# A two-layer decoder trunk on one core: index scores and mixer A's values merged into fewer stages, powers alone on GpSimd

## The chip, the cores and the metric

The kernel runs on one core of a Trainium2 chip. The metric is the device time of one execution in microseconds (us), the median of several runs; lower is better. The granted TensorE clock in the profiled execution is 0.999 of full speed.

## The reference, cut to what matters

Two decoder layers work on 256 positions of width 1024. One layer is:

```
u    = RMSNorm(h)
proj = u @ w_in  -> qa ka va | qi ki wi | qb kb vb | gate_a gate_b
mixer A: iscore = sum_h wi_h * relu(qi_h . ki)   (4 index heads of 64, causal)
         sel    = the 64 best keys of each query
         softmax(qa . ka) over sel, times va       (8 heads of 64, one shared key and value)
mixer B: softmax(q1 . k1) - lam * softmax(q2 . k2), times vb, per-head RMSNorm (4 heads)
h   += (sigmoid(gate_a) * (o_a @ w_a) + sigmoid(gate_b) * (o_b @ w_b)) @ w_out
h   += ConvFFN(RMSNorm(h))                       (2816 wide, causal width 3, GELU gate)
h   += sigmoid(RMSNorm(h) @ w_ple_gate) * (p @ w_ple_proj)
```

The norms inside the mixers (of qa, ka, qb, kb per head, and of mixer B's output per head) are x * (mean(x^2) + eps)^(-1/2).

## The kernel before, in words

The 256 positions are two tiles of 128 (i = 0, 1). Every weight matrix is cut into chunks of 128 x 1024 floats, 128 chunks per layer, which stream in on the SP queue. ScalarE copies a chunk into a rounded high part `wh` (`split_hi`, line 164) and VectorE subtracts to get the low part `wl` (`split_lo`, line 179; in most of the up-projection GpSimd does half of it, line 176). A product is three TensorE products: high times high, high times low, low times high. `gemm_a` (line 337) runs a projection of 512 columns: for each of the eight blocks of the contraction it issues six products (three for each tile) at line 361.

The attention work is hidden between these products. It is written as generators ("threads") that each issue one stage and then yield three numbers: what the stage is charged on TensorE, VectorE and ScalarE. `Side` (line 61) is a planner that runs while the program is written out, not on the chip. `gemm_a` calls `tick` after every two contraction blocks, so after twelve products, which are charged 2.6 us. One tick goes through the threads by priority and skips a thread whose last stage is not yet due (`t[2]`), skips all of them when the planned VectorE is more than 3.5 us behind (`LIMIT_US`), and issues no further stage once the tick's charges on TensorE have passed 2 us (`SIDE_US`, line 86). After the threads, `tick` prepares further weight chunks. All engines execute in the order in which the program issues, so the plan fixes each engine's queue. `side.until` runs threads with no projection between them until a flag is set.

The threads that the change touches, per layer:

- `index_side` (line 493): rotary products for the index heads, transposes, then for each tile one stage of index scores: four products of 64 contraction rows (line 528, two trace instructions to a pair of row halves), two Relu copies (line 531), and a yield. After both, `select_side` is spawned: the weighted sums and the top-64 mask, on VectorE.
- `heads_side` (line 568): rotary products and norms of qb, kb, qa for each tile. `head_ss` (417) squares on ScalarE and sums on VectorE; `rpow` (260) gives (mul * ss + add)^(-1/2) on GpSimd with two instructions, a multiply-add (263) and a power (264).
- `mixer_b` (641), four of them: score maps, normalisation, transposes, products with the values (662), then the output norm: two squares on ScalarE (667), two multiplications by 1/sum on VectorE (670), `rpow` (672), another multiplication by 1/sum (674), and the scaled output (675).
- `mixer_a` (687), four of them in the order `ORDER_A` = (0,1), (1,1), (0,0), (1,0) of (half of the heads, tile): score maps (602, 639), division by the sums (695), transposes (`ptrans`, 626), then as a last stage of its own the products with the values (705) and the split of the result into high and low parts of `o` (709, 710).
- `nxt_side` (970), once, in the last projection of layer 0: transposes (317) of the first half of `h` for the next layer.

PSUM has four accumulators for the projections (`ps_acc`) and four buffers for all side work (`ps_tp`).

After the four gate projections come the two products of mixer B's output with `w_branch_b` (line 754, four ticks in all), then `side.until` for mixer A's flags (755), then the products with `w_branch_a` (768), which read `o` of mixer A.

Of the kernel before, what the change touches and what calls it, by code (L numbers as in the profile page):

```python
# [9 lines left out]
F32 = mybir.dt.float32  # L10
F32R = mybir.dt.float32r
BF16 = mybir.dt.bfloat16
AF = mybir.ActivationFunctionType
ALU = mybir.AluOpType
# [3 lines left out]
P = 128  # L18
L = 256
# [6 lines left out]
EPS = 1e-6  # L26
# [31 lines left out]
NONE = (0.0, 0.0, 0.0)  # L58
# [51 lines left out]
def decoder_kernel(ctx: ExitStack, tc: tile.TileContext, x, xa, pT, ws, fc, tb, gf, rope, out):  # L110
    nc = tc.nc
# [4 lines left out]
    sm = ctx.enter_context(tc.tile_pool(name="sm", bufs=2))  # L116
    T2 = dict(tag="t2", bufs=10)
    ps_acc = ctx.enter_context(tc.tile_pool(name="ps_acc", bufs=4, space=PSUM))
    ps_tp = ctx.enter_context(tc.tile_pool(name="ps_tp", bufs=4, space=PSUM))
    ctx.enter_context(tc.manual_schedule())  # L120
    side = Side()
# [135 lines left out]
    nc.gpsimd.tensor_copy(cmb, cm[:, P:])  # L257


    def rpow(dst, src, mul, add):  # L260
        n = src.shape[-1]
        t = sm.tile([P, 8], F32, name="pw", bufs=4)
        nc.gpsimd.tensor_scalar(t[:, :n], src, mul, add, op0=ALU.mult, op1=ALU.add)
        nc.gpsimd.tensor_tensor(dst, t[:, :n], mhalf[:, :n], op=ALU.pow)  # L264

    def sq_half(ss, hf, tiles=(0, 1)):

# [61 lines left out]
    def split_T_side(srcs, hf, scale, x, flag):  # L329
        for k0 in (0, 2):  # L330
            split_T2(srcs, hf, k0, scale, x)
            yield 0.45, 0.8, 0.3
        flags.add(flag)

    flags = set()
# [78 lines left out]
        else:  # L414
            nc.vector.tensor_add(dst, m1, m2)

    def head_ss(src, n):
        sq = sm.tile([P, 8, 64], F32, name="sq", **T2)[:, :n, :]
        ss = sm.tile([P, 8], F32, name="hss", bufs=3)
        nc.scalar.activation(sq, src, AF.Square)  # L420
        nc.vector.reduce_sum(ss[:, :n], sq, axis=AX.X)
        return ss[:, :n]

    def transposed(srcs, nb, dst):
# [23 lines left out]
    for l in range(DEPTH):  # L448
# [44 lines left out]
        def index_side(pi):  # L493
            kk, iq, wvs = [], [], []
            for i in range(2):
                v = pi[i]
                nc.scalar.activation(va[:, i, :], v[:, 64:128], AF.Copy)
                kki = sm.tile([P, 4, 64], F32, name="kk")
                rope_rows(kki[:, 0:2, :], v[:, 0:64].unsqueeze(1), 1, rt["ka"], i, dup=True)
                rope_rows(kki[:, 2:4, :], v[:, 384:448].unsqueeze(1), 1, rt["i"], i, dup=True)  # L500
                rk = sm.tile([P, 1], F32, name="rk")
                rpow(rk, head_ss(v[:, 0:64].unsqueeze(1), 1), 1.0 / 64, EPS)
                iqi = sm.tile([P, 4, 64], F32, name="iq")
                rope_rows(iqi, v[:, 128:384].rearrange("p (a b) -> p a b", b=64), 4, rt["i"], i)
                nc.scalar.activation(kki[:, 0:2, :], kki[:, 0:2, :], AF.Copy, scale=rk)
                wv = sm.tile([P, 4], F32, name="wv")
                nc.vector.tensor_scalar(wv, v[:, 448:452], 0.0625, None, op0=ALU.mult)
                kk.append(kki.rearrange("p a b -> p (a b)"))
                iq.append(iqi.rearrange("p a b -> p (a b)"))
                wvs.append(wv)  # L510
                yield 0.0, 2.8, 0.0
            pt = ps_tp.tile([P, 2, L], F32, name="tp")
            for j in range(2):
                for i in range(2):
                    nc.tensor.transpose(pt[:, j, i * P:(i + 1) * P], kk[i][:, j * P:(j + 1) * P], ident)
            nc.scalar.activation(kT, pt[:, 0, :], AF.Copy)
            nc.scalar.activation(kiT, pt[:, 1, :], AF.Copy)
            iqT = sm.tile([P, 2, L], F32, name="iqT", **T2)
            transposed(iq, 2, iqT)
            yield 0.9, 0.0, 1.2  # L520
            rels = []
            for i in range(2):
                S = P * (i + 1)
                rel = b4("rel")[:, :, :S]
                ps = [ps_tp.tile([P, 2, L], F32, name="tp") for _ in range(2)]
                for b in range(2):
                    for r in range(2):
                        nc.tensor.matmul(ps[r][:, b, :S], iqT[r * 64:(r + 1) * 64, b, i * P:(i + 1) * P],
                                         kiT[r * 64:(r + 1) * 64, :S], start=True, stop=True)
                for r in range(2):  # L530
                    nc.scalar.activation(rel[:, r:4:2, :], ps[r][:, :, :S], AF.Relu)
                rels.append(rel)
                yield 0.85 * (i + 1), 0.0, 0.9
            side.spawn(select_side(rels, wvs), P_TOPK)

        def select_side(rels, wvs):
# [31 lines left out]
        def heads_side(pr, nm, is_q):  # L568

            rows, rq = [], []  # L570
            for i in range(2):
                v = pr[i].rearrange("p (a b) -> p a b", b=64)
                q = sm.tile([P, 512], F32, name="qr", **T2)
                q3 = q.rearrange("p (a b) -> p a b", b=64)
                r_ = sm.tile([P, 8], F32, name="rq", bufs=6)
                if is_q:
                    rope_rows(q3, v, 8, rt[nm], i)
                    rpow(r_, head_ss(v, 8), 1.0, 64 * EPS)
                else:
                    rpow(r_, head_ss(v, 8), 1.0 / 64, EPS)  # L580
                    rope_rows(q3, v, 8, rt[nm], i)
                    nc.vector.tensor_mul(q3, q3, r_.unsqueeze(2).broadcast_to([P, 8, 64]))
                rows.append(q)
                rq.append(r_.rearrange("p (b r) -> p r b", r=2))
                yield 0.0, (2.8 if nm == "kb" else 2.2), 0.0
            rqs[nm] = rq
            qT[nm] = b4("qT")
            transposed(rows, 4, qT[nm])
            yield 0.9, 0.0, 1.0
            flags.add(nm)  # L590
# [50 lines left out]
        def mixer_b(hq, i):  # L641
# [5 lines left out]
            cf = sm.tile([P, 2], F32, name="cf", bufs=4)  # L647
            nc.vector.reciprocal(rcp, sums)
            nc.vector.scalar_tensor_tensor(cf, rcp[:, 1, :], nlam, sums[:, 0, :], op0=ALU.mult, op1=ALU.mult)
            for m in range(2):  # L650
                nc.vector.scalar_tensor_tensor(pe[:, 2 * m, :], pe[:, 2 * m + 1, :], cf[:, m:m + 1],
                                               pe[:, 2 * m, :], op0=ALU.mult, op1=ALU.add)
# [11 lines left out]
            sq = sm.tile([P, 2, P], F32, name="osq", **T2)  # L664
            ss_ = sm.tile([P, 2], F32, name="oss")
            for m in range(2):
                nc.scalar.activation(sq[:, m, :], po[:, m, :], AF.Square, accum_out=ss_[:, m:m + 1])
            r1 = rcp[:, 0, :]
            for _ in range(2):
                nc.vector.tensor_mul(ss_, ss_, r1)  # L670
            ff = sm.tile([P, 2], F32, name="ff")
            rpow(ff, ss_, 1.0 / P, EPS)
            yield 0.4 * (i + 1), 0.5, 1.6
            nc.vector.tensor_mul(ff, ff, r1)
            nc.vector.tensor_mul(ob[:, i, hq * 256:(hq + 1) * 256].rearrange("p (b c) -> p b c", c=P), po,
                                 ff.unsqueeze(2).broadcast_to([P, 2, P]))
            yield 0.0, 0.4, 0.0
# [9 lines left out]
        def mixer_a(hq, i):  # L687
            while not {"qa", "mask"} <= flags:
                yield NONE
            pe, sums = maps("qa", product_a, i, hq, mask[i])  # L690
            yield 0.9 + 0.9 * i, 0.8 + 0.6 * i, MA + MB * i
            rcp = sm.tile([P, 2, 2], F32, name="rcp", bufs=4)
            nc.vector.reciprocal(rcp, sums)
            for hh in range(4):
                nc.vector.tensor_scalar(pe[:, hh, :], pe[:, hh, :], rcp[:, hh % 2, hh // 2:hh // 2 + 1], None,
                                        op0=ALU.mult)
            yield 0.0, 0.9 + 0.3 * i, 0.0
            pt = ptrans(pe, 4, i)
            yield 0.5 + 0.5 * i, 0.0, 0.5 + 0.5 * i
            nb = i + 1  # L700
            ptv = pt[:, :4 * nb, :].rearrange("p (m r s) t -> p m r s t", r=2, s=nb)
            po = ps_tp.tile([P, 2, L], F32, name="tp")[:, 0, :].rearrange("p (m t) -> p m t", t=P)
            for sb in range(nb):
                for r in range(2):
                    nc.tensor.matmul(po[r * 64:(r + 1) * 64], va[:, sb, :], ptv[:, :, r, sb, :],  # L705
                                     start=sb == 0, stop=sb == i)
            x = o_parts()
            hi, lo = x.two(2 * hq, slice(i * P, (i + 1) * P))
            nc.scalar.activation(hi, po, AF.Copy)
            nc.vector.tensor_sub(lo, po, hi.bitcast(F32))  # L710
            yield 0.85 * nb, 0.4, 0.35
            flags.add(("a", hq, i))

        def o_side():
            while not {("b", hq, i) for hq, i in ORDER_B} <= flags:
# [17 lines left out]
        side.spawn(heads_side(project(C_QA, 512, "q"), "qa", True), 0)  # L733
        for hq, i in ORDER_A:
            side.spawn(mixer_a(hq, i), 1)


        tg = {}
# [227 lines left out]
        if not last:  # L966
            nxt, nss = HL("u"), new_ss()
            g_nxt = fcs[l + 1][:, 0:8]

            def nxt_side():  # L970
                yield from split_T_side([h[:, i, HALF[0]] for i in range(2)], 0, lambda k: g_nxt[:, k:k + 1],
                                        nxt, "n0")
                sq_half(nss, 0)
                yield 0.0, 0.0, 1.1
# [100 lines left out]
```

## Time and profile before

| | |
|---|---|
| time, median of 3 runs (lowest to highest) | 789.85 us (788.91 to 790.34) |
| the profiled execution: time | 788.69 us |
| its span, first to last instruction | 786.9 us |
| TensorE busy | 779.7 us (99%) |
| VectorE busy | 588.6 us (75%) |
| ScalarE busy | 501.3 us (64%) |
| GpSimd busy | 162.7 us (21%) |

Busy shares are unions of instruction times. A product's row in the timeline has its start and its duration; products overlap, so the distance from one start to the next is what a product costs in a stream, and the duration is longer. PE is TensorE, DVE is VectorE, ACT is ScalarE, POOL is GpSimd.

### The profile page before, as it was taken

What the parts mean: (1) busy time and instruction counts of PE and PEld (TensorE: products, weight loads), DVE (VectorE), ACT (ScalarE), POOL (GpSimd) and SP (SyncE); (2) the same over time, 40 slices, a digit from 0 to 9 for tenths busy, and PEclk for the clock granted to TensorE, in tenths of its full rate; (3) what the DMA queues carried; (4) which work ended last, traced back from release to release, by engine and by line L of the source; (5) the groups of instructions that cost most, each with busy time, mean ns of one, the idle gap of its engine ahead of it and who ended that gap; (6) DMA issues with size and microseconds to landing.
All of it is one profiled execution on the core that took longest, in us unless ns stands there. A gap on an engine that the chain in (4) does not pass through costs nothing.

```text
span 786.9 us, 11698 instructions
## 1 busy us (share of the span) xinstructions
PE 779.7 (99%) x4034; PEld 648.1 (82%) x4034; DVE 588.6 (75%) x1128; ACT 501.3 (64%) x886; POOL 162.7 (21%) x162
## 2 busy tenths in 40 slices
PE   9999999999999999999999999999999999999997
PEld 7877886788888888888888778778888888888886
DVE  5987997675887778754687889768668878795643
ACT  5776657455877777553576486565468777773541
POOL 0250300001344442000123213000104444400000
PEclk9999999999999999999999999999999999999999
DMA  9654353462665556656465345445636656558521
GB/s 331 229 174 152 123 193 125 149 228 94 213 211 180 198 192 210 229 162 224 134 195 177 125 142 166 147 135 189 209 119 207 204 176 202 180 180 290 172 96 54
DMA packets 40204, 140.04 MB, mean 178 GB/s; under 512 B 4560, under 2 KB 5200, under 8 KB 40144
## 3 DMA queue, kind: packets, MB, share of 16 engines
q1 hardware_dynamic: 39280, 137.44, 52.8%
q10 hardware_dynamic: 864, 1.84, 0.7%
q8 instruction: 32, 0.52, 0.3%
q14 instruction: 28, 0.23, 0.1%
HBM read 138.22 MB, written 1.05 MB: 177 GB/s over the span
## 4 chain that ended last, share of the span: by engine, by line
PE 91%; DVE 3%; ACT 3%; POOL 1%; issue 1%; DVEq 0%; ACTq 0%
PE acc L361 36%; PE tp L831 21%; PE tp L833 11%; PE acc L932 5%; PE acc L934 5%; PE acc L933 5%; ACT pe L611 2%; PE tp L317 2%; DVE wl L179 2%; PE tp L626 1%; PE tp L705 1%; PE tp L662 1%; PE tp L639 1%; POOL rq L264 1%; PE tp L431 1%
## 5 line engine op out<-in xcount | busy, mean ns | idle before, releaser
L164 ACT ACTIVATE wh<-raw 128x1024 fp32r<-128x1024 f32 x254 | 263.9, 1057 | 38.4 <-PE acc L934 23.4
L179 DVE TENSOR_TENSOR wl<-raw,wh 128x1024 fp32r<-128x1024 f32 x178 | 213.8, 1220 | 27.8 <-ACT wh L164 27.5
L361 PE MATMUL acc<-wh,u 128*128 128x512 f32 (+1 forms) x672 | 215.1, 394 | 0.0
L831 PE MATMUL tp<-u,wh 128*128 128x512 f32 x704 | 177.1, 392 | 0.0
L361 PEld LDWEIGHTS acc<-wh,u 128*128 128x128 f32 x672 | 126.3, 189 | 26.7 <-issue 0.7
L831 PEld LDWEIGHTS tp<-u,wh 128*128 128x128 f32 x704 | 126.3, 189 | 22.3
L361 PE MATMUL acc<-wl,u 128*128 128x512 f32 (+1 forms) x336 | 129.3, 389 | 0.2 <-DVE wl L179 0.2
L176 POOL TENSOR_TENSOR wl<-raw,wh 128x512 fp32r<-128x512 f32 x76 | 98.5, 1296 | 142.8 <-ACT wh L164 60.9
L833 PEld LDWEIGHTS tp<-u,wl 128*128 128x128 f32 x704 | 96.6, 190 | 7.2
L833 PE MATMUL tp<-u,wl 128*128 128x256 f32 x704 | 98.8, 282 | 0.0
L865 DVE SCALAR_TENSOR_TENSOR cv<-tp,fc,cv 128x255 f32<-128x255 f32 (+1 forms) x176 | 84.2, 478 | 3.1
L361 PEld LDWEIGHTS acc<-wl,u 128*128 128x128 f32 x336 | 63.1, 188 | 12.5 <-DVE wl L179 1.0
L860 DVE TENSOR_TENSOR tp<-tp,cl 128x256 f32<-128x256 f32 x88 | 38.0, 432 | 45.8 <-ACT cl L858 45.4
L932 PE MATMUL acc<-wh,g 128*128 128x512 f32 x176 | 68.9, 391 | 0.0
L934 PE MATMUL acc<-wh,g 128*128 128x512 f32 x176 | 68.5, 389 | 0.0
L933 PE MATMUL acc<-wl,g 128*128 128x512 f32 x176 | 68.5, 389 | 0.0
L861 ACT ACTIVATE cv<-tp,fc 128x256 f32<-128x256 f32 x88 | 49.7, 565 | 25.8 <-DVE tp L860 25.3
L278 POOL TENSOR_SCALAR sst<-ss 128x2 f32<-128x2 f32 (+1 forms) x8 | 5.6, 698 | 259.8 <-ACT junk L270 259.6
L175 DVE TENSOR_TENSOR wl<-raw,wh 128x514 fp32r<-128x514 f32 x76 | 53.6, 705 | 0.0
L858 ACT ACTIVATE cl<-tp 128x256 f32<-128x256 f32 x88 | 33.6, 382 | 28.7 <-PE tp L833 28.6
L611 ACT ACTIVATE pe<-tp,nb,rq 128x256 f32<-128x256 f32 (+1 forms) x64 | 31.8, 528 | 18.0 <-DVE nb L608 12.2
L361 PE MATMUL acc<-wh,o 128*128 128x512 f32 x128 | 42.5, 399 | 0.0
(174 smaller groups left out, 946.4 us busy)
## 6 DMA issues: line engine op xcount, KB each, us to landing
raw<-ws SPq DMA_DIRECT2D x254, 512.0 KB, 3.5
raw<-ws SPq DMA_DIRECT2D x4, 256.0 KB, 5.1
h<-x SPq DMA_DIRECT2D x2, 512.0 KB, 7.1
gb<-gf ACTq DMA_DIRECT2D x2, 512.0 KB, 4.7
out<-h SPq DMA_DIRECT2D x3, 256.0 KB, 2.0
x<-xa SPq DMA_DIRECT2D x2, 256.0 KB, 3.9
px<-pT ACTq DMA_DIRECT2D x2, 256.0 KB, 2.7
tbl<-tb SPq DMA_DIRECT2D x1, 256.0 KB, 6.9
```

Source lines behind the costliest of these rows:

```text
L164: nc.scalar.activation(wh, raw, AF.Copy)
L175: nc.vector.tensor_sub(wl[:, a], raw[:, a], wh[:, a].bitcast(F32))
L176: nc.gpsimd.tensor_tensor(wl[:, b], raw[:, b], wh[:, b].bitcast(F32), op=ALU.subtract)
L179: nc.vector.tensor_sub(wl, raw, wh.bitcast(F32))
L361: nc.tensor.matmul(acc[i][:, :n], a, w, start=q == 0 and j == 0, stop=q == nk - 1 and not any(t[0] == i for t in todo[n_ + 1:]))
L831: nc.tensor.matmul(acc, wh[:, k, :], u.pair(k), start=k == 0, stop=False)
L833: nc.tensor.matmul(acc[:, 0, :], wl[:, k, :], u.hi(k), start=False, stop=k == KD - 1)
L861: nc.scalar.activation(c, pu, AF.Identity, bias=w[:, 3:4], scale=w[:, 2:3])
L865: nc.vector.scalar_tensor_tensor(c[:, sh:], pu[:, :L - sh], w[:, 2 - sh:3 - sh], c[:, sh:], op0=ALU.mult, op1=ALU.add)
L932: nc.tensor.matmul(acc[i], a, wh, start=k == 0, stop=False)
L933: nc.tensor.matmul(acc[i], a, wl, start=False, stop=False)
L934: nc.tensor.matmul(acc[i], b, wh, start=False, stop=k == NF - 1)
```

## The change

Four edits, in both layers except the last:

1. `rpow` keeps only the power on GpSimd. Its multiply-add goes: the factor moves into the scale of the square on ScalarE, the addend is a new small VectorE addition in `head_ss`. In `mixer_b` the factor moves into the square as well; the two multiplications by 1/sum and the one after the power go, and instead eps * sum^2 is worked out once and added to the sum of squares.
2. `index_side` issues the scores of both tiles and yields once.
3. `mixer_a` ends with its transposes. A new thread `values_a(i)`, one per tile, waits for both halves of the heads and issues all their products with the values, then the splits.
4. `nxt_side` yields once, charged 2.8 us of VectorE, before its first transposes.

```diff
-    def rpow(dst, src, mul, add):
-        n = src.shape[-1]
-        t = sm.tile([P, 8], F32, name="pw", bufs=4)
-        nc.gpsimd.tensor_scalar(t[:, :n], src, mul, add, op0=ALU.mult, op1=ALU.add)
-        nc.gpsimd.tensor_tensor(dst, t[:, :n], mhalf[:, :n], op=ALU.pow)
+    def rpow(dst, src):
+        nc.gpsimd.tensor_tensor(dst, src, mhalf[:, :src.shape[-1]], op=ALU.pow)
...
-    def head_ss(src, n):
+    def head_ss(src, n, scale, eps):
...
-        nc.scalar.activation(sq, src, AF.Square)
+        nc.scalar.activation(sq, src, AF.Square, scale=scale)
         nc.vector.reduce_sum(ss[:, :n], sq, axis=AX.X)
+        nc.vector.tensor_scalar(ss[:, :n], ss[:, :n], eps, None, op0=ALU.add)
...
                 rels.append(rel)
-                yield 0.85 * (i + 1), 0.0, 0.9
+            yield 2.1, 0.0, 1.8
...
+            es = sm.tile([P, 2], F32, name="es", bufs=4)
+            nc.vector.scalar_tensor_tensor(es, sums[:, 0, :], EPS, sums[:, 0, :], op0=ALU.mult, op1=ALU.mult)
...
-                nc.scalar.activation(sq[:, m, :], po[:, m, :], AF.Square, accum_out=ss_[:, m:m + 1])
-            r1 = rcp[:, 0, :]
-            for _ in range(2):
-                nc.vector.tensor_mul(ss_, ss_, r1)
+                nc.scalar.activation(sq[:, m, :], po[:, m, :], AF.Square, scale=P ** -0.5, accum_out=ss_[:, m:m + 1])
+            nc.vector.tensor_add(ss_, ss_, es)
             ff = sm.tile([P, 2], F32, name="ff")
-            rpow(ff, ss_, 1.0 / P, EPS)
+            rpow(ff, ss_)
             yield 0.4 * (i + 1), 0.5, 1.6
-            nc.vector.tensor_mul(ff, ff, r1)
...
             yield 0.5 + 0.5 * i, 0.0, 0.5 + 0.5 * i
+            pts[hq, i] = pt
+        pts = {}
+        def values_a(i):
+            while not {(0, i), (1, i)} <= set(pts):
+                yield NONE
             nb = i + 1
...
+            for hq in range(2):
+                ptv = pts[hq, i][:, :4 * nb, :].rearrange("p (m r s) t -> p m r s t", r=2, s=nb)
+                po = ps_tp.tile([P, 2, L], F32, name="tp")[:, 0, :].rearrange("p (m t) -> p m t", t=P)
+                for sb in range(nb):
+                    for r in range(2):
+                        nc.tensor.matmul(po[r * 64:(r + 1) * 64], va[:, sb, :], ptv[:, :, r, sb, :],
+                                         start=sb == 0, stop=sb == i)
+                pos.append(po)
             x = o_parts()
+            for hq in range(2):
+                hi, lo = x.two(2 * hq, slice(i * P, (i + 1) * P))
+                nc.scalar.activation(hi, pos[hq], AF.Copy)
+                nc.vector.tensor_sub(lo, pos[hq], hi.bitcast(F32))
+            yield 1.3 * nb, 0.8, 0.35
+            for hq in range(2):
+                flags.add(("a", hq, i))
...
         for hq, i in ORDER_A:
             side.spawn(mixer_a(hq, i), 1)
+        for i in (1, 0):
+            side.spawn(values_a(i), 1)
...
             def nxt_side():
+                yield 0.0, 2.8, 0.0
                 yield from split_T_side([h[:, i, HALF[0]] for i in range(2)], 0, lambda k: g_nxt[:, k:k + 1],
```

## Rows read from the trace of the kernel before

**Rows 1.** The page: TensorE's busy time, and the chain by engine.

```profile
PE 779.7 (99%) x4034; PEld 648.1 (82%) x4034; DVE 588.6 (75%) x1128; ACT 501.3 (64%) x886; POOL 162.7 (21%) x162
...
PE 91%; DVE 3%; ACT 3%; POOL 1%; issue 1%; DVEq 0%; ACTq 0%
```

**Rows 2.** Two stretches: width, busy us of PE, PEld, DVE, ACT, POOL.

```profile
80.00:100.00 20.00, 20.00 (x111) 16.94 (x110) 19.55 (x60) 13.35 (x30) 7.38 (x9) 1.00 0.40 132
760.00:787.00 27.00, 22.59 (x127) 19.53 (x125) 12.27 (x19) 7.64 (x15) 1.97 (x3) 0.96 0.11 40
```

**Rows 3.** Timeline of PE, layer 0's index scores: start us, us, instruction.

```profile
40.79 0.39 PE L361 MATMUL acc<-wl,u 128*128 128x512 f32 x1
41.01 0.39 PE L361 MATMUL acc<-wh,u 128*128 128x512 f32 x1
41.33 0.72 PE L528 MATMUL tp<-kiT,iqT 64*128 64x128 f32 x8
41.98 0.50 PE L361 MATMUL acc<-wh,u 128*128 128x512 f32 x1
42.31 0.39 PE L361 MATMUL acc<-wl,u 128*128 128x512 f32 x1
...
44.61 0.39 PE L361 MATMUL acc<-wh,u 128*128 128x512 f32 x1
44.92 1.13 PE L528 MATMUL tp<-kiT,iqT 64*128 64x256 f32 x8
45.99 1.09 PE L431 MATMUL tp<-ident,qr 128*128 128x128 f32 x8
```

**Rows 4.** Timeline of PE, layer 0's mixer A: transposes and products with values.

```profile
128.79 1.03 PE L626 MATMUL tp<-ident,pe 128*128 128x128 f32 x8
...
137.41 1.08 PE L705 MATMUL tp<-pt,va 128*64 128x256 f32 x8
138.43 0.66 PE L626 MATMUL tp<-ident,pe 128*128 128x128 f32 x4
...
145.69 0.65 PE L705 MATMUL tp<-pt,va 128*64 128x256 f32 x4
146.27 0.50 PE L361 MATMUL acc<-wh,o 128*128 128x512 f32 x1
146.61 0.39 PE L361 MATMUL acc<-wl,o 128*128 128x512 f32 x1
```

**Rows 5.** Timeline of PE where it waits: idle and releaser in brackets.

```profile
61.06 0.98 PE L431 MATMUL tp<-ident,qr 128*128 128x128 f32 x7 [0.21 <-DVE qr L582]
...
125.07 0.27 PE L602 MATMUL tp<-mk,identb 128*128 128x256 bf16 x1 [0.48 <-ACT pe L611]
...
386.44 0.93 PE L317 MATMUL tp<-ident,h 128*128 128x128 f32 x4
```

**Rows 6.** Instructions by line: count | busy us, mean ns | idle before.

```profile
L263 POOL TENSOR_SCALAR pw<-hss 128x8 f32<-128x8 f32 (+1 forms) x16 | 11.3, 708 | 99.5 <-DVE hss L421 79.5 <-DVE rcp L648 20.0
L670 DVE TENSOR_TENSOR oss<-oss,rcp 128x2 f32<-128x2 f32 x16 | 2.4, 158 | 0.9 <-ACT osq L667 0.6
L649 DVE SCALAR_TENSOR_TENSOR cf<-rcp,nlam,sums 128x2 f32<-128x2 f32 x8 | 1.8, 224 | 0.3
L551 DVE MAX8 m<-sc 128x8 f32<-128x128 f32 (+1 forms) x32 | 9.8, 349 | 0.0
L553 DVE MATCH_REPLACE8 sc<-m,sc 128x128 f32<-128x128 f32 (+1 forms) x32 | 10.7, 344 | 0.0
```

**Rows 7.** Timeline of DVE and PE: a low part, and its first use.

```profile
82.34 1.22 DVE L179 TENSOR_TENSOR wl<-raw,wh 128x1024 fp32r<-128x1024 f32 x1
...
85.39 0.39 PE L361 MATMUL acc<-wl,u 128*128 128x512 f32 x1
```

**Rows 8.** Timeline: the last split of mixer A's output in layer 0.

```profile
146.81 0.42 DVE L710 TENSOR_TENSOR o<-tp,o 128x256 fp32r<-128x256 f32 x1 [0.32 <-ACT o L709]
```

More of the change, by code (lines that the diff above doesn't have):

```diff
@@ L501, in index_side @@
                 rk = sm.tile([P, 1], F32, name="rk")
-                rpow(rk, head_ss(v[:, 0:64].unsqueeze(1), 1), 1.0 / 64, EPS)
+                rpow(rk, head_ss(v[:, 0:64].unsqueeze(1), 1, 0.125, EPS))
                 iqi = sm.tile([P, 4, 64], F32, name="iq")
@@ L577, in heads_side @@
                     rope_rows(q3, v, 8, rt[nm], i)
-                    rpow(r_, head_ss(v, 8), 1.0, 64 * EPS)
+                    rpow(r_, head_ss(v, 8, 1.0, 64 * EPS))
                 else:
-                    rpow(r_, head_ss(v, 8), 1.0 / 64, EPS)
+                    rpow(r_, head_ss(v, 8, 0.125, EPS))
                     rope_rows(q3, v, 8, rt[nm], i)
@@ L699, in mixer_a @@
             yield 0.5 + 0.5 * i, 0.0, 0.5 + 0.5 * i
-            nb = i + 1
[L701 to L706, printed above, removed]
-            x = o_parts()
[L708 to L712, printed above, removed]
+            pts[hq, i] = pt
[3 more added lines that the diff above has]
+                yield NONE
+            nb = i + 1
+            pos = []
+            for hq in range(2):
[6 more added lines that the diff above has]
+                pos.append(po)
+            x = o_parts()
+            for hq in range(2):
[5 more added lines that the diff above has]
+                flags.add(("a", hq, i))
         def o_side():
```

## The prediction

> **What bounds the kernel now.** I read the page first. TensorE is busy 779.7 us, 99% of the span, and 91% of the chain that ended last is TensorE [rows 1]; the reader is to see that no other engine's work sets the time, and that an edit pays only where TensorE's own queue gets shorter. Next the stretches: of the 7.2 us in which TensorE is idle (786.9 - 779.7), 4.4 lie in the last 27 us [rows 2], which no edit touches. But a product's duration there overlaps the next one's, so busy time doesn't show a product that starts late. Third, therefore, the timeline of TensorE, read by distances between starts. In a stream of products of 512 columns it is 0.22 to 0.23 us; I take 0.227. Where side work comes between two of them the distances grow, and that is what this change moves.
>
> **Merged index scores.** In [rows 3] tile 0's stage begins 0.32 us after the last projection product (41.01 to 41.33), so 0.09 late; its eight instructions take 0.65; the first product behind it takes 0.33 (41.98 to 42.31), 0.10 too long. Tile 1's stage is again 0.09 late and takes 1.07; eight transposes follow it at once. Their group lasts 1.09, against 1.03 for the same eight begun straight from the projection [rows 4], so 0.06. What a pair of products costs in the stream comes from the values stages [rows 4]: four pairs in 1.02 us (137.41 to 138.43), two pairs in 0.58 (145.69 to 146.27), so 0.22 a pair and 0.14 fixed per stage. A pair of index scores of tile 1 has as many columns, one of tile 0 half: the fixed parts are 0.65 - 4 x 0.11 = 0.21 and 1.07 - 4 x 0.22 = 0.19. One stage less saves 0.09 + 0.20 + 0.06 = 0.35 us per layer. The least is 0.15 (the fixed part stays), the most 0.40 (a way out to the projection goes, 0.10). I take 0.35.
>
> **Merged values.** Before there are four stages per layer, after it two. Two ways in and two fixed parts go: 2 x (0.09 + 0.14) = 0.46. Ways out: before, three lead to transposes (0.06 each) and one to the projection (146.27 to 146.61, 0.34, so 0.11): 0.29; after, two lead to the projection: 0.22. That saves 0.07, together 0.53 per layer, least 0.25 (fixed parts stay), most 0.60.
>
> A rule of the Trainium skill bears on this (TensorEngine Tiling (Array Packing), Key Properties): changing the tiling mode, not just the tile, drains TensorE. The trace agrees that something of the kind is paid at each such border, 0.09 us on the way in. The rule prices only the drain, though; with the 128 cycles that TensorE: Matmul & The Clock Gate gives for a drain (Step-by-step: what each phase is for), an estimate of 0.05 us, the twelve borders that go in two layers would be worth 0.6 us.
>
> Where does the plan put the new stages? By line 86 no further stage is issued once a tick's charges pass 2. In the products with `w_branch_b` a tick before held values (1.7) and one transpose stage (1.0), which passes 2, so each of its four ticks held one values stage, the last just ahead of `w_branch_a`. After the change tile 1's second half (1.0) and both halves of tile 0 (0.5 each) fit in the first of these ticks, tile 1's values (2.6) are alone in the next, tile 0's (1.3) in the third. At least twelve products then stand between the last values and their reader, as now, and the splits stay hidden: the last one ends at 147.23 [rows 8], 0.96 us behind its products (146.27, rows 4), against 2.7 us of twelve products.
>
> By the same sums layer 0 shifts: the index stage charges 2.1, the kb heads start one tick earlier, selection and mixer A's maps follow one or two ticks earlier. Mixer A's score maps there spread over three ticks instead of two, one more way out to the projection: 0.11 us lost. Nothing shows that it can be more than two (0.2).
>
> **Powers alone on GpSimd.** The 24 multiply-adds go; the 16 in the heads cost 708 ns each [rows 6]. VectorE loses 16 multiplications of 158 ns and eight like them (24 x 0.158 = 3.8 us) and gains eight eps terms (as line 649, 224 ns: 1.8), eight additions (1.3) and 16 in `head_ss` (2.5): +1.8 us on 588.6. It has idle time everywhere but in the stretch of selection, where it is busy 19.55 of 20 us [rows 2]. Low parts are made ahead of their use: one made by 83.56 is used at 85.39 [rows 7], 1.83 us of cover, against about 0.9 us more VectorE work per layer, spread. So the work itself costs nothing, and if that cover is gone at most 0.9 per layer. The latency of a power falls by 0.708 - 0.158 = 0.55 us; this counts only where TensorE waits for it, which is the transposes behind `qr` at 61.06, 0.21 us [rows 5].
>
> **Later transposes.** At 386.44 four transposes last 0.93 us [rows 5], against 0.66 for four behind a values stage [rows 4]: 0.27 more, which I read as a wait for `h`. With the yield (2.8 on VectorE, due 3.3 later) the next tick, 2.6 later, is skipped, the pairs go out in the third and fourth ticks. The last pair then stands just before the next layer's index projection, which needs it only twelve products later (each a little shorter there). In between VectorE must finish the gate's four operations and this pair's two low parts, an order that no row shows; so I bound this edit by a gain of 0.27 and a loss of 0.5 (one VectorE operation too many, 0.42 in [rows 8], with its hand-over), and take the gain: the reader's first two products of that block need only the high part, which ScalarE makes.
>
> **Waits.** TensorE's wait for a score map's buffer, 0.48 at 125.07 [rows 5], comes from four maps in two adjoining ticks; spread over three it goes. With 0.21 and 0.27 that makes 0.96 us. New orders bring new waits; the rows show waits of 0.2 to 0.5, so I set two against it, 0.46. Net 0.5, bounds -1.0 (four of 0.48) and +0.96.
>
> **Sum.** 2 x (0.35 + 0.53) = 1.76 for the merged stages, less 0.11, plus 0.5: 2.15 us less. The profiled execution took 788.69 us, 1.16 below the median of the runs; I apply the difference to both: 786.5 for it, 787.7 for the median of 789.85.
>
> **Rivals.**
> A, the fixed part stays. Each group of heads or tile pays its 0.14 or 0.20 inside a merged stage as well, since its first weights are new ones. Then a merge saves only ways in and out: 0.15 + 0.25 per layer, 0.8 in all; with half of the net waits less the extra way out, about 1.0: 788.9, no change. For it: I have no row of two such groups back to back. Against it: in the values stage of four pairs the block of values changes half-way at no visible cost. The skill's rule, named above, would give nearly the same time by its small price.
>
> B, the time comes back as waits. A merged stage fills more of the four side buffers at once (index scores all four), and their evictions queue on ScalarE; the next transposes or maps wait. For it: TensorE's waits before are of this kind, 0.48 at 125.07. Against it: twelve products (2.7 us) lie between ticks. At two to four new waits of 0.48 the gain falls by 1.0 to 1.9 beyond the sum: 788.7 to 789.6, no change.
>
> C, slower: VectorE in selection. The earlier start moves top-64 rounds (lines 551, 553) ahead of low parts while their lead is smallest. A stage of rounds takes (9.8 + 10.7) / 8 = 2.6 us, lead 1.83 [rows 6, 7]: TensorE waits 0.77 at each collision, plus up to 0.9 of added VectorE work per layer. It decides where the lead of a low part falls under one stage of rounds, and the time is slower than before from five such collisions on: 3.85 - 2.15, 791.5. All eight stages, with the 1.8 of added work, cost 8.0, less the 2.15: 795.7. For it: 19.55 of 20 us. Against it: VectorE has room just before, where the work moves to, and the weights lead more in most of the stretch.
>
> D, the plan doesn't do it: tile 0's values come out last, directly before `w_branch_a`. Its first product then waits for the high part, ready at about 146.81 for products done by 146.27 [rows 4, 8], 0.54 us, in both layers 1.1: 788.8, no change. My own addition of the ticks speaks against it.
>
> **How the numbers follow.** About 0.2% (1.6 us) is what a measurement of this kernel can tell from no change. Forecast 0.56, A 0.12, B 0.14, C 0.10, D 0.08. The forecast's own range is 786.8 to 788.3 (a sum from 1.6 to 3.0; at its most the merges give 2.0 and the waits 0.96). C alone is slower (0.10); A, B and D are no change (0.34), from which a part (0.01) reaches over the bound: faster 0.57, no change 0.33, slower 0.10. The range is stretched over A, B and D, and by the 0.5 to 0.9 by which single runs before lie from their median: 786.2 to 790.5, which leaves C out above and little below.
>
> **What would show it.** Right: eight score pairs as one group of line 528 per layer of about 1.5 us with one late start; values in two groups of line 705 per layer (about 1.9 and 1.0 us), followed by twelve products or more before `w_branch_a`; no idle bracket at the qb or kb transposes. A: groups 0.14 to 0.2 longer than that. B: idle of TensorE on side buffers, released by ScalarE, above 1 us in all. C: idle of TensorE before a `wl` product, released by line 179. D: idle at the first product of `w_branch_a`. I am wrong if TensorE's idle time outside the last 27 us, now 7.2 - 4.4 = 2.8 us, rises by more than 1 us, or if the distance around the merged stages does not shrink.

## The result, and the profile after

The changed kernel takes 798.65 us (797.97 to 798.99, 4 runs) against 789.91 (788.91 to 790.34, 4 runs) for the kernel before beside it: ratio 1.0114 [1.0102, 1.0127], by the ratio 9.0 us slower. I had said 787.7 (786.2 to 790.5), and faster with a chance of 0.57. The profiled execution took 798.46 us with a span of 796.6; before it was 788.69 and 786.9.

From the page after, busy time by engine and the chain by engine, to be read against [rows 1]:

```profile
PE 783.1 (98%) x4034; PEld 652.7 (82%) x4034; DVE 589.8 (74%) x1136; ACT 501.4 (63%) x886; POOL 156.4 (20%) x138
...
PE 90%; DVE 5%; ACT 3%; issue 1%; POOL 1%; DVEq 0%; ACTq 0%; POOLq 0%
```

The number of TensorE's instructions is the same, yet it is busy 3.4 us longer and idle 13.5 instead of 7.2 us, and VectorE has 5% of the chain instead of 3%. So two things happened: TensorE waited, and some of its instructions became longer. TensorE's waits after (us in total, times, longest):

```profile
PE tp L601 <- ACT pe L610: 3.7, 5, 2.4
PE tp L601 <- DVE o L318: 2.0, 1, 2.0
PE tp L430 <- DVE qr L581: 1.4, 1, 1.4
...
PE acc L358 <- DVE wl L179: 0.7, 2, 0.6
```

Line 601 opens a score map (the mask's product into a side buffer), line 610 is the exp that frees such a buffer, line 318 the second part of the split of mixer B's output `o`, line 430 the transposes of the heads, line 581 the kb heads' last multiplication. The timeline of TensorE shows where (the bracket is the idle time before and its releaser):

```profile
59.38 0.88 PE L430 MATMUL tp<-ident,qr 128*128 128x128 f32 x6 [1.40 <-DVE qr L581]
...
452.51 1.14 PE L633 MATMUL tp<-qT 64*128 64x256 f32 x8
...
457.21 0.39 PE L358 MATMUL acc<-wh,u 128*128 128x512 f32 x1
459.98 0.31 PE L601 MATMUL tp<-cmb,identb 128*128 128x256 bf16 x1 [2.38 <-ACT pe L610]
461.07 0.37 PE L601 MATMUL tp<-cmb,identb 128*128 128x256 bf16 x1 [0.78 <-ACT pe L610]
461.37 2.08 PE L633 MATMUL tp<-qT 64*128 64x256 f32 x8
...
504.33 0.60 PE L314 MATMUL tp<-ident,ob 128*128 128x128 f32 x4
504.77 0.48 PE L601 MATMUL tp<-mk,identb 128*128 128x256 bf16 x2
...
506.07 0.27 PE L601 MATMUL tp<-mk,identb 128*128 128x256 bf16 x1 [0.18 <-ACT pe L610]
508.38 0.37 PE L601 MATMUL tp<-mk,identb 128*128 128x256 bf16 x1 [2.04 <-DVE o L318]
```

There are three places: one in layer 0 at 59, two in layer 1 at 457 to 461 and 506 to 508. And the windows around the two in layer 1 (width, busy us of PE, of TensorE's weight loads PEld, of DVE, ACT and POOL, then the granted clock and what the DMA moved):

```profile
457.00:461.00 4.00, 0.90 (x4) 0.36 (x3) 3.54 (x8) 2.28 (x9) 0.00 (x0) 0.88 0.43 147
461.00:466.00 5.00, 4.93 (x21) 3.08 (x21) 2.24 (x6) 4.82 (x15) 0.00 (x0) 0.50 0.35 108
466.00:470.00 4.00, 4.00 (x17) 3.18 (x17) 3.24 (x6) 4.00 (x16) 0.00 (x0) 0.89 0.41 127
...
505.00:508.50 3.50, 1.28 (x12) 0.71 (x10) 0.89 (x3) 2.54 (x6) 0.00 (x0) 0.91 0.43 150
508.50:514.50 6.00, 6.00 (x20) 4.63 (x20) 3.88 (x11) 3.96 (x17) 0.00 (x0) 0.50 0.17 46
514.50:518.00 3.50, 3.50 (x22) 3.01 (x22) 1.07 (x3) 3.50 (x7) 0.00 (x0) 0.97 0.18 73
```

After each of the two the clock is at 0.50, the lower of its two levels (1.2 GHz), for 5 and 6 us, where it was 1.00 in the 5 us ahead (452 to 457, 500 to 505). TensorE is busy 99 and 100% there, at about half the pace: the eight products of line 633 that take 1.14 us at 452.51 take 2.08 at 461.37. That is where the longer instructions come from. (The Trainium skill, TensorE: Matmul & The Clock Gate, "A second HAM failure mode: psum-queue depth-cycling", tells of a kernel that idles between groups while it cycles through its result buffers, and whose clock goes up and down for it; the two stretches of 0.50 behind waits for side buffers agree.)

The account in us, from these rows: idle 2.38 + 0.78, 0.18 + 2.04 and 1.40, together 6.8. Half a clock over 4.93 and 6.00 us of work is 5.46, the partly slow windows beside them add 0.77 (0.11 x 4.00, 0.12 x 0.90, 0.09 x 1.28, 0.03 x 3.50): 6.2. Lost 13.0, and the spans differ by 9.7, so the change gained some 3.3 elsewhere. The kernel of x9 below, which does the same work without these waits, bears the two sums out: 6.3 us less idle time (7.2) and 6.2 us less busy time (776.9).

What delayed the buffers is on VectorE and ScalarE. VectorE's timeline:

```profile
449.02 0.61 DVE L550 MAX8 m<-sc 128x8 f32<-128x128 f32 x2
...
453.64 0.61 DVE L550 MAX8 m<-sc 128x8 f32<-128x128 f32 x2
...
455.99 1.22 DVE L179 TENSOR_TENSOR wl<-raw,wh 128x1024 fp32r<-128x1024 f32 x1
457.12 1.28 DVE L606 TENSOR_REDUCE mx<-tp 128x2 f32<-128x512 f32 x2
...
507.58 0.75 DVE L318 SCALAR_TENSOR_TENSOR o<-tp,gsub,o 128x512 fp32r<-128x512 f32 x1 [3.40 <-ACT o L317]
```

In the kernel before, from the timelines of TensorE and VectorE, the same products, their reduce and the first rounds of layer 1:

```profile
450.08 1.13 PE L634 MATMUL tp<-qT 64*128 64x256 f32 x8
...
451.40 1.28 DVE L607 TENSOR_REDUCE mx<-tp 128x2 f32<-128x512 f32 x2
...
462.38 0.61 DVE L551 MAX8 m<-sc 128x8 f32<-128x128 f32 x2
```

ScalarE's timeline after:

```profile
458.72 0.56 ACT L610 ACTIVATE pe<-tp,nb,rq 128x256 f32<-128x256 f32 x1 [7.48 <-DVE nb L607]
...
505.89 1.08 ACT L164 ACTIVATE wh<-raw 128x1024 fp32r<-128x1024 f32 x1
506.83 0.71 ACT L317 ACTIVATE o<-tp,gsub 128x512 fp32r<-128x512 f32 x1
```

First place: the products of mixer B's first map are done by 453.65, but two stages of top-64 rounds (from 449.02 and 453.64, 2.4 us each) with low parts among them stand ahead of its `reduce_max` (line 606, 457.12, 3.5 us behind the products; before it was 0.2 us); the exps start at 458.72, and the next maps need the buffers that these free. Second place: `o`'s transposes (504.33) and two maps of mixer A fall into one tick and want five side buffers of four; the eviction of `o` (506.83) stands on ScalarE behind eight exps (from 501.54 on) and a high part, the buffer is free after line 318, at 508.3. Third: the kb transposes of layer 0 run a tick earlier than before, and their heads are not ready.

The merged stages themselves did what was forecast. TensorE's timeline in layer 0, against [rows 3] and [rows 4]:

```profile
41.24 0.39 PE L358 MATMUL acc<-wh,u 128*128 128x512 f32 x1
41.56 1.58 PE L527 MATMUL tp<-kiT,iqT 64*128 64x128 f32 x16
43.07 0.50 PE L358 MATMUL acc<-wh,u 128*128 128x512 f32 x1
...
135.34 1.95 PE L713 MATMUL tp<-pt,va 128*64 128x256 f32 x16
137.22 0.50 PE L358 MATMUL acc<-wh,o 128*128 128x512 f32 x1
...
140.16 1.08 PE L713 MATMUL tp<-pt,va 128*64 128x256 f32 x8
141.17 0.50 PE L358 MATMUL acc<-wh,o 128*128 128x512 f32 x1
```

Sixteen score products take 1.51 us from start to the next product (before 0.65 + 1.07), sixteen with the values 1.88 (before 2 x 1.02), eight 1.01 (before 2 x 0.58).

### The profile page after: what moved, and what is told of

Read it like the earlier page. It is cut to its first block, busy times and chain, and to the rows that moved or that the text cites. A ratio compares the mean times of both kernels' runs of the same rounds, so it can differ in the third digit from the quotient of the medians.

```text
span 796.6 us, 11680 instructions
## 1 busy us (share of the span) xinstructions
PE 783.1 (98%) x4034; PEld 652.7 (82%) x4034; DVE 589.8 (74%) x1136; ACT 501.4 (63%) x886; POOL 156.4 (20%) x138
## 3 DMA queue, kind: packets, MB, share of 16 engines
q10 hardware_dynamic: 864, 1.84, 0.7%
## 4 chain that ended last, share of the span: by engine, by line
PE 90%; DVE 5%; ACT 3%; issue 1%; POOL 1%; DVEq 0%; ACTq 0%; POOLq 0%
PE acc L358 35%; PE tp L844 20%; PE tp L846 11%; PE acc L945 5%; PE acc L947 5%; PE acc L946 5%; DVE wl L179 2%; ACT pe L610 2%; PE tp L314 1%; PE tp L625 1%; PE tp L638 1%; PE tp L713 1%; PE tp L663 1%; DVE mx L606 1%; POOL rq L261 1%
## 5 line engine op out<-in xcount | busy, mean ns | idle before, releaser
L358 PE MATMUL acc<-wh,u 128*128 128x512 f32 (+1 forms) x672 | 217.6, 398 | 0.0
L261 POOL TENSOR_TENSOR rq<-hss,mhalf 128x8 f32<-128x8 f32 x12 | 27.6, 2296 | 94.7 <-DVE hss L420 70.3
```

Source lines behind the costliest of these rows:

```text
L358: nc.tensor.matmul(acc[i][:, :n], a, w, start=q == 0 and j == 0, stop=q == nk - 1 and not any(t[0] == i for t in todo[n_ + 1:]))
```

## The experiments

My theory: the single charge of 2.1 for the index scores, where two stages were charged 0.85 and 1.7, lets the planner start the selection a tick earlier; everything behind it is placed anew, and that costs the time. Rivals: the added VectorE work, the stages of the values with their buffers, or the merged stage itself. Eleven kernels ran; each ratio is to the kernel before on the same chip. The first four start from the changed kernel.

**x1, index scores back in two stages.**

```diff
                 rels.append(rel)
-            yield 2.1, 0.0, 1.8
+                yield 0.85 * (i + 1), 0.0, 0.9
```

> The changed kernel with the index scores in two stages again (edits 1, 3 and 4 stay). Theory 'early rounds': the merged stage's charge of 2.1 lets selection start earlier in layer 1, so that two stages of top-64 rounds stand on VectorE ahead of mixer B's first score maps, and mixer A's maps fall together with o_side. Undone, both long waits of TensorE (3.2 and 2.2 us) and the half-clock stretches behind them (about 2.6 and 3.1 us lost) go: 787.5 us, 786.5 to 788.5. Rival 'added VectorE work': the 24 new small VectorE operations, or the values kept for later, make the waits: stays at 795 or above.

Measured: 787.2 us, ratio 0.9982 [0.9973, 0.9991]. Both long waits are gone, and no transposes of heads wait. All the loss hangs on this one line, and the other three edits together gain 1.4 us.

**x2, the top-64 rounds held back until the kb heads are done** (in `select_side`).

```diff
+            while "kb" not in flags:
+                yield NONE
             m8 = [sm.tile([P, 8], F32, name=f"m8{i}", bufs=1) for i in range(2)]
```

> The changed kernel, all four edits, but select_side holds its top-64 rounds back until the kb heads are flagged. Early rounds: 787.2 us, 786.3 to 788.3, both long waits gone with the merged stage still in place. Rival 'side buffers': the merged stages fill the four PSUM side buffers and that makes the waits: stays at 796 or above.

Measured: 790.01 us, ratio 1.0023 [1.0014, 1.0032]: a miss. The waits at 457 and 506 are gone, so both hang on the early rounds, but a line of TensorE's waits is left that I had not counted:

```profile
PE tp L430 <- DVE qr L583: 3.3, 2, 1.9
```

The kb transposes now wait in both layers, 1.40 and 1.87 us. The early index stage moves the kb heads too.

**x3, half of the top-64 rounds left out** (the first of each pair), so the mask is another one.

```diff
-                for i in range(2):
+                for i in range(2 if rnd % 2 else 0):
                     nc.vector.max(m8[i], scs[i])
-                for i in range(2):
+                for i in range(2 if rnd % 2 else 0):
                     nc.vector.match_replace(scs[i], m8[i], scs[i], SENT)
```

> The changed kernel with only four of the eight top-k rounds per layer (32 keys are marked, so the mask is another one), the order of all else as it was. Early rounds: each stage of rounds ahead of mixer B's maps is half as long, so about 2.4 us less stand before them; the first wait (3.16 us) falls below 1 and its half-clock stretch goes; the second wait, of mixer A's maps with o_side, stays: 793, 791.5 to 794.5. Side buffers: 798.

Measured: 793.94 us, ratio 1.0067. The order is unchanged, the first wait shrinks, the second stays:

```profile
PE tp L601 <- DVE o L318: 2.0, 1, 2.0
PE tp L601 <- ACT pe L610: 1.6, 5, 0.8
```

So the length of the rounds in front of the reduce sets the first wait, and the second does not hang on the first.

**x4, mixer A's maps of tile 0 not before mixer B's output is split.**

```diff
-            while not {"qa", "mask"} <= flags:
+            while not {"qa", "mask"} <= flags or (i == 0 and "ob" not in flags):
```

> The changed kernel with mixer A's maps of tile 0 held back until o_side is done, so that o_side's transposes and four buffers of maps are not in one tick. The second wait (2.2 us) and its half-clock stretch (about 3.1 us lost) go, the first stays: 793.3, 792 to 794.5. Rival: the second wait is only a late consequence of the first (exponentials pushed back on ScalarE) and comes up elsewhere: 797 or above.

Measured: 793.39 us, ratio 1.006. Now the second wait is gone and the first stays (a new one of 0.8, on line 693, takes a small part back); with x3, the two places are independent:

```profile
PE tp L601 <- ACT pe L610: 3.4, 3, 2.4
```

**x5 to x8, each edit alone on the kernel before.** x5 has the index stage of the change, x6 `values_a` and its two spawns, x7 the powers, x8 this:

```diff
             def nxt_side():
+                yield 0.0, 2.8, 0.0
```

> The kernel before with the merged index scores alone. My theory (the one charge of 2.1 moves the selection ahead of the kb heads and of mixer B's first maps) puts the same order into layer 1 as in the changed kernel, so both long waits of TensorE come back here, on the score maps behind the exps (about 3 us in two) and on the buffers that o's split frees (about 2 us), each followed by some 5 us at half the clock: 797 to 800 us. The rival that the stages of the values or the added work of VectorE are needed for the loss gives less than half of it: 788 to 793.

> The kernel before with the merged values alone. By the terms of my prediction it saves 0.53 us a layer, 1.06 in all, and the wait of 0.48 for a map's buffer may go or stay: 787.2 to 788.0 beside a kernel before at 788.6. If each group pays its fixed part inside the merged stage too, 0.5: 788.1. If a merged stage brings waits of its own: 788.6 or more.

> The kernel before with the powers alone on GpSimd (multiply-adds gone there, the constants moved to ScalarE's scale and to VectorE). By my sum VectorE's 1.8 us are hidden and the wait of 0.21 behind qr goes: within 0.3 us of before, 788.3 to 788.9. If VectorE is the bound in selection: up to 1.8 us slower, 790.4.

> The kernel before with the later start of the next layer's transposes alone. By my prediction 0.27 us less, bounds a gain of 0.27 and a loss of 0.5: 788.3, at most 789.1.

Measured: index scores alone 798.67 us, ratio 1.0126 [1.0109, 1.0143]; values alone 787.34, 0.9982 [0.9973, 0.9991]; powers alone 788.61, 1.0001 [0.9992, 1.001]; later transposes alone 788.5, 0.9997 [0.9988, 1.0006]. In us at 788.7 that is +9.9, -1.4, +0.1 and -0.2, in sum +8.4, beside 9.0 for all. TensorE's waits in x5 are those of the change again:

```profile
PE tp L602 <- ACT pe L611: 4.0, 4, 2.8
PE tp L602 <- DVE o L321: 2.0, 1, 2.0
PE tp L431 <- DVE qr L582: 2.0, 2, 1.6
```

Neither the values nor the added VectorE work is needed for the loss.

**x9, the merged stage with the old charges.** All scores are issued at once, and an empty stage follows.

```diff
-            yield 2.1, 0.0, 1.8
+            yield 0.85, 0.0, 0.9
+            yield 1.7, 0.0, 0.9
```

> The changed kernel, its index scores of both tiles issued in one stage as in the change, but charged to the planner as the two stages before (0.85, then an empty stage of 1.7). All else is placed as in the run where the index scores were undone (787.2 us). If only the placement costs and the merged stage itself saves the 0.35 us a layer of my prediction, 786.5 us, faster than before by 2.1. If the merged stage costs something itself (all four side buffers filled at once, a wait on ScalarE's evictions): 787.2 or more.

Measured: 786.47 us, ratio 0.9962 [0.9949, 0.9974]: faster than before by 3.0 us, and the best version here. The stage is merged as in the change; only what the planner is told differs (two yields for one), and 12 us go. TensorE's waits on score maps are those of before again, 0.9 us in three. From its page:

```profile
PE 776.9 (99%) x4034; PEld 648.6 (83%) x4034; DVE 589.7 (75%) x1136; ACT 500.8 (64%) x886; POOL 156.4 (20%) x138
```

TensorE's timeline: the qb transposes of layer 0 (the first row), and the products of mixer B's first map in layer 1, done by 449.03:

```profile
45.65 1.03 PE L430 MATMUL tp<-ident,qr 128*128 128x128 f32 x8
...
447.89 1.14 PE L634 MATMUL tp<-qT 64*128 64x256 f32 x8
```

VectorE there: the reduce follows at once, the rounds come only at 460.12:

```profile
449.15 1.28 DVE L607 TENSOR_REDUCE mx<-tp 128x2 f32<-128x512 f32 x2
...
460.12 0.62 DVE L551 MAX8 m<-sc 128x8 f32<-128x128 f32 x2
```

**x10, x2 with the kb transposes a tick later.**

```diff
-                yield 0.0, (2.8 if nm == "kb" else 2.2), 0.0
+                yield 0.0, (3.6 if nm == "kb" else 2.2), 0.0
```

> The changed kernel with the top-64 rounds held back until the kb heads are done, and with 3.6 instead of 2.8 charged to VectorE for a stage of kb heads, which puts the kb transposes one tick later in both layers. Without the second part 790.0, with two waits of the kb transposes for qr, 1.40 and 1.87 us. If these waits are all that was left of the loss, they go and the time is 790.0 - 3.3 = 786.7. If the heads are only late because VectorE has too much to do, the waits move to the first maps and it stays at 789 to 790.

Measured: 786.96 us, ratio 0.997 [0.9959, 0.9981], as expected: the kb waits were what was left of the loss in x2. Two different ways to restore the order thus end within half a microsecond of each other.

**x11, the charge of the merged stage at 1.9.**

```diff
-            yield 2.1, 0.0, 1.8
+            yield 1.9, 0.0, 1.8
```

> The changed kernel with 1.9 charged for the merged index stage instead of 2.1, so that the tick goes on to the qb heads behind it and nothing of the heads slips. If what costs is the head pushed out of its tick by a charge above 2, both long waits go: about 786.5. If what costs is that the selection starts a tick earlier (one stage is done where two were wanted), two stages of rounds still stand ahead of mixer B's maps in layer 1, and both waits with the slow clock behind them stay; only the wait of the kb transposes in layer 0 goes: 796 to 798. I expect this one.

Measured: 795.55 us, ratio 1.0073 [1.0053, 1.0092], half a microsecond below the range that I gave it. The wait for `o` stays, the kb wait of layer 0 goes, a wait of 0.9 at its qb transposes (44.48) is new, and that on the maps comes in two pieces:

```profile
457.56 0.27 PE L601 MATMUL tp<-cmb,identb 128*128 128x256 bf16 x1 [0.79 <-ACT pe L610]
458.65 0.27 PE L601 MATMUL tp<-cmb,identb 128*128 128x256 bf16 x1 [0.82 <-ACT pe L610]
```

So it is not that 2.1 passes the planner's limit of 2; the stage being done in one tick instead of two is enough to let the selection in early.

## Why the prediction was wrong, step by step

**What bounds the kernel, merged scores, merged values: right.** Scores: before the group 0.09 late, as before (41.24 to 41.56); in it 1.72 - 1.51 = 0.21 saved, one way in 0.09, one way out 0.06 (the transposes of x9 last 1.03, not 1.09): 0.36 per layer against 0.35. Values: 0.16 + 0.15 in the two groups, two ways in 0.18, ways out 0.07: 0.56 against 0.53, and alone 1.4 us against 1.06. Rival A (the fixed part stays) is out. The estimate of 0.6 us from the Trainium skill's drain (TensorEngine Tiling (Array Packing), Key Properties) is too small: 2 x 0.92 = 1.8 by these rows, 0.15 us for each of the twelve borders. What is paid there beyond the estimate no run separates.

**Powers: no change that can be told, as said.** VectorE has 1.2 us more work (588.6 to 589.8), not 1.8, and it is hidden; the wait of 0.21 behind `qr` is gone in x7. The fall of 0.55 in the latency was mis-sized: for the kb heads, which TensorE waits for, it is 0.13, as the last section shows.

**Later transposes: right.** Four of them last 0.60 us (at 392.26) where they took 0.93 [rows 5], 0.33 against my 0.27; alone -0.2 us, less than can be told from nothing.

**Where the plan puts the stages: this step failed.** I added up the ticks for the values, right in all, and for layer 0, and closed with "Mixer A's score maps there spread over three ticks instead of two [...]: 0.11 us lost. Nothing shows that it can be more than two (0.2)." I did not follow the selection through layer 1, where the heads slip (qb transposes at 434.03, before 428.68), the first weighted sum of the selection starts at 430.44 (before 438.59), so the rounds pass mixer B's first maps, and `o`'s transposes meet two maps of mixer A; nor did I ask in layer 0 whether the kb heads, started a tick earlier, are ready: they are not, by 1.40 us. The planner moves a whole chain when one charge changes, and I priced only the piece that I looked at. The sign that I had named for being wrong came: TensorE's idle time outside the last stretch rose by far more than 1 us.

**Waits: the term was mis-sized for the same reason.** I set two new waits of 0.23 against three that go. Of the three, the 0.48 shrank to 0.16 (at 123.42), the 0.27 went, and that behind `qr` grew to 1.40; with the two places in layer 1 it came to 6.8 us idle and 6.2 at the lower clock level. The sizes of waits in the trace of before (0.2 to 0.5) say what its own order leaves, not what another order brings; the two new ones in layer 1 come from the work that they queue behind (two stages of rounds of 2.4 each, eight exps and a high part). Of the lower clock the sum had no term.

**The rivals.** B had the place (side buffers, released by ScalarE), but sized at 0.48 each. C had the cause (rounds on VectorE, too early), but let them collide with the low parts: these cost little (line 179 releases 0.7 us of waits, before 0.2 in one wait). Both halves were there; I didn't join them: what VectorE's rounds delay is the reduce that begins a buffer's release. D didn't happen. Without the failed step the sum comes out: x9 lies at -3.0 us [-4.0, -2.05] by its ratio, which takes in my 2.15. In part that is luck: between the profiled executions (spans 786.9 and 784.1) the 2.8 us are all busy time, idle time is 7.2 in both, so the 0.5 net that I took from waits is not there as idle time; the rows above name 1.84 for the merged stages and 0.33 for the later transposes, and the other 0.6 no run separates.

## What to carry to other kernels

Where a planner places work by charges, a merged stage is two edits: what it does and what it tells the planner. Follow the changed order to the end of the layer before pricing it, and ask at each moved stage which buffer's release stands behind it. Merging stages and keeping the old charges (x9) gives the gain without the rest; and a wait of 2 us on TensorE cost some 4 here (x4).

## What the hardware showed that I had not expected

**A wait can cost more than its length when the clock falls, and not every wait makes it fall.** The wait of 2.04 for `o`, with the 0.18 ahead of it and the slow clock behind, stands at 5.4 us in the account above; taking it away (x4) gave back 1.0114 - 1.006, some 4.3 us, with a new wait of 0.8 in place. In x2 the profiled execution waited 1.87 us at 446, and the clock stayed at 1.00 (columns as above, TensorE alone):

```profile
448.00:450.00 2.00, 2.00 (x13) 1.00 0.21 49
```

In x11 the two waits of 0.79 and 0.82 with a product between them were followed by 0.50:

```profile
461.00:464.00 3.00, 3.00 (x13) 0.50 0.03 5
```

In x3 the same 0.18 and 2.04 as in the changed kernel were followed by a slow stretch of about half the length, 1.7 us lost (0.27 x 6 + 0.01 x 6) instead of 3:

```profile
502.00:508.00 6.00, 4.61 (x19) 0.73 0.01 2
508.00:514.00 6.00, 5.63 (x34) 0.99 0.28 87
```

The order of the instructions alone does not decide it. Of x11's four executions two had a mean granted clock of 1.000 (793.93 and 794.45 us) and two 0.993 (796.64 and 796.92), 2.6 us apart; of x2's eleven, seven had 1.000 (789.4 to 790.1) and four 0.996 to 0.998 (791.1 to 791.7). Of the changed kernel's four, one had 0.996 against 0.990 to 0.993, and it was only 0.5 to 1.0 us shorter (797.97). So the 6.2 us are what the lower clock added to the profiled execution; that the kernel would gain as much if the clock stayed up is not shown, and in x11 most of the loss is there at 1.000 too (7.5 and 8.0 us above x9). What decides whether the clock falls, and for how long, was not tried.

**A power on GpSimd took longer when its multiply-add was gone.** The powers of 128x8, before and after (count, then busy us and the mean of one in ns):

```profile
L264 POOL TENSOR_TENSOR rq<-pw,mhalf 128x8 f32<-128x8 f32 x12 | 22.8, 1899 | 1.0
```

```profile
L261 POOL TENSOR_TENSOR rq<-hss,mhalf 128x8 f32<-128x8 f32 x12 | 27.6, 2296 | 94.7 <-DVE hss L420 70.3
```

The same operation takes 2.30 us on average instead of 1.90. The multiply-add of line 263 took 0.85 in this shape (the 0.708 of [rows 6] mixes in four of 0.295 in another), so almost half of what its removal saved went again. The new VectorE addition takes its part too: from the start of VectorE's sum of squares to the end of the power, the kb heads of layer 0 took 3.11 us before and take 2.98 after, the qb heads 4.45 and 3.52. No run here tells why the power itself is longer.
